# Adding the last two experts' rows in SBUF by one-hot products instead of by scatters to DRAM

## The chip, the cores and the metric

One Trainium2 chip, of which the kernel uses one core. The metric is device time in microseconds (us). Three runs of the kernel before took 2404.68, 2408.65 and 2410.79 us; their median, 2408.65 us, is the time that a change is compared with.

## The reference

Two layers of a diffusion backbone on 512 latent tokens of 1024 channels. The part that matters is the end of the second layer: every token goes to 2 of 8 experts, each expert is a SwiGLU with 3584 hidden units, the results times their gates are added to the stream, and a last norm follows.

```python
top_logit, top_idx = lax.top_k(logits, TOP_K)
gates = jax.nn.softmax(top_logit, axis=-1)
...
hid = jax.nn.silu(xb @ w1[e]) * (xb @ w3[e])
return (hid @ w2[e]) * w[:, None]
...
out = jnp.zeros_like(xt).at[buf_tok].add(y.reshape(P, shp[-1]))
...
x = x + g2 * ffn(h_l)
...
return rmsnorm(x, final_g)
```

All arithmetic is float32. The kernel makes a float32 product of three fast products of the operands' high and low parts.

## The kernel before

The experts are sorted by their number of tokens and have fixed places for 192, 160, 160, 144, 128, 128, 128 and 128 tokens. They are worked on in four pairs: rank 0 with rank 4, 1 with 5, 2 with 6, 3 with 7. In the text the larger expert of a pair is the one of more than 128 tokens, in the last pair 144, and the smaller one has 128.

The weights of an expert stream in blocks of about 1 MB on SP's queue into four buffers `raw`. ScalarE (ACT) rounds each half of a block to its high part `hi`, VectorE (DVE) subtracts to get the low part `lo` (`split`, L165 to L167); each of `hi` and `lo` has five half-block buffers. TensorE (PE) multiplies these. A generator per expert yields after each block, and `weave` takes the generators by turns: first the hidden units (28 blocks for each expert), then the outputs, `outputs` for the smaller expert (14 blocks, called units below, of two 128-row slabs of w2) and `outputs_t` for the larger one (16 steps: four column blocks of 256, each in four steps). The smaller expert comes first in each round, so that the larger one has its last two steps alone.

`outputs` ends with a multiplication by gate and g2 into `yt` (L1339) and a scatter. `outputs_t` ends each column block with a sum of two PSUM halves (`both`, L1287 and L1288), a transposition (`transposed_y`, L1363) and the same multiplication (L1364); after the last column block it issues two scatters, for tokens 0 to 127 and for the 16 that are left. A scatter (L1315) is an indirect DMA of GpSimd (POOL) that adds rows to the stream `xd` in DRAM; the scatters wait for each other.

After the four pairs stands a loop over blocks of tokens beyond the fixed places (L1432), whose count is read from SBUF (L1431). Then `final` (L1452 to L1468) reads the stream back from `xd` in four tiles of 128 tokens, takes squares, root, reciprocal and the product with `final_g`, and writes each tile to the output. A scheduler sets the order of the instructions on each engine, so that the text of the program isn't that order; each engine then works through its own queue in order.

Of the kernel before, what the change touches and what calls it, by code (L numbers as in the profile page):

```python
# [10 lines left out]
F32 = mybir.dt.float32  # L11
# [25 lines left out]
# columns of the constant table  # L37
# [27 lines left out]
# parameters with a value for every channel, as columns of 128 channels  # L65
# [7 lines left out]
def layout(inputs):  # L73
    """The arrays of the launch: the inputs, the parameters as columns, the streams channel-major too, and the constants"""
# [7 lines left out]
    arrays["consts"], arrays["rope"] = const_tables()  # L82
    return arrays


class Net:
# [26 lines left out]
    def slot(self, whole=False):  # L113
        """Buffers (raw, high part, low part) of the next block of the weight stream, by turns; only the raw one if `whole`"""
# [17 lines left out]
    def load(self, src, a, b):  # L132
        """A weight block [128, a, b] (a*b <= 2048): its high and low parts for the fast float32 products."""
# [9 lines left out]
        # in pieces, so that what others wait for can come between  # L143
# [5 lines left out]
    def mm3(self, ps, terms, segs, first=True, last=True):  # L149
        """ps[:, seg] = sum over terms of (wh + wl)^T (xh + xl), without wl^T xl."""  # L150
# [10 lines left out]
    def stream(self, tag, dt, name):  # L161
        """A [128, 8, tokens] tile for the latent tokens and one for the context tokens"""
        return [self.big.tile([P, KT, n], dt, tag=f"{tag}{v}", name=f"{name}{v}") for v, n in enumerate((L, C))]
# [6 lines left out]
    def start(self):  # L170
# [19 lines left out]
        # conditioning vectors: for every k-tile columns (lat, ctx) and zeros, the stationary operand of a quarter of the array  # L190
# [25 lines left out]
    def load_z(self, ss, t):  # L216
        """A tile of x or ctx over its root mean squares, channel-major"""
# [9 lines left out]
    def turn(self, dst, src, t):  # L227
        """A tile of tokens into its place in a channel-major stream"""
# [9 lines left out]
    def first_norm(self, k):  # L238
        """h of layer 0 from the normalised streams, for the channels of k-tile k"""
# [8 lines left out]
    def ada(self, l, t, m=4, before=None, tags=None):  # L248
        """128 m columns of the modulation of layer l from 128 t, in four sums (k-tile modulo 4), in a quarter of the array each"""
# [24 lines left out]
    def columns(self, l, t, m, sums, nv):  # L274
        """Columns t ... of the modulation from their sums and the bias, and the scales times the gains"""
# [40 lines left out]
    def mod(self, l, which):  # L316
        """columns [128, 8, 2] of chunk `which` (sh1, sc1, g1, sh2, sc2, g2) of layer l"""
        return self.acol[l][:, 8 * which:8 * which + 8, :]

    def inv_rms_cols(self, sq, n, d, pool):  # L320
        """1 / sqrt(mean + eps) of the d squares of each of n tokens, whose sums over the partitions of sq [128, n]
        are the squares' sums, as columns of 128 tokens"""
# [9 lines left out]
    def spread(self, r, n, pool):  # L332
        """Columns of 128 tokens as n columns, on every partition"""
# [10 lines left out]
    def norm(self, l, which, seg, pool, out=None, full=None, between=None, tags=None):  # L344
        """The parts of the modulated norm of the stream, for one segment of tokens, into out (or HH, HL)"""
# [27 lines left out]
    def residual(self, k, ps, gate, segs):  # L373
        """x += gate * ps for the channels of k-tile k"""
# [5 lines left out]
    def softplus_cols(self):  # L380
        """n4 = -4 * softplus(-lam), p4 = 4 * softplus(-lam): [128, 16] columns"""
# [10 lines left out]
        V.tensor_tensor(x, x, lam, op=ALU.min)                       # -|lam|  # L392
# [10 lines left out]
        V.tensor_scalar(q, q, 1.0, None, op0=ALU.add)                # exp(f)  # L403
# [914 lines left out]
    def outputs(self, X):  # L1318
# [4 lines left out]
        for u in range(nf // 2):  # L1323
# [10 lines left out]
            if f < nf - 1:  # L1334
                yield
# [203 lines left out]
```

## Time and profile before

| what | value |
|---|---|
| median of three runs | 2408.65 us |
| span of the profiled execution | 2406.2 us |
| PE busy | 2331.3 us, 97% |
| DVE busy | 1733.8 us, 72% |
| ACT busy | 1333.9 us, 55% |
| POOL busy | 43.1 us, 2% |
| HBM read | 477.04 MB |

The profiled execution has no time of its own beside its span; the span, from its first to its last instruction, stands 2.45 us under the median. A matmul counts as busy until its result is written, so that neighbours overlap, and its duration is longer than the distance from one start to the next. "Idle before" is time in which the engine did nothing, and the name behind the arrow is what ended it.

### The profile page before, as it was taken

The numbers are of one execution on the slowest core, as the hardware profiler recorded it, in microseconds if no ns is written. First come the engines' busy times: TensorE is split into PE (matmuls) and PEld (weight loads), VectorE is DVE, ScalarE is ACT, GpSimd is POOL, SyncE is SP. The second block draws the span as 40 slices with busy tenths as digits, with TensorE's granted clock in tenths as the row PEclk, the third lists the DMA queues.
The fourth block names the chain that finished last, engine by engine and source line by source line (L and its number), as shares of the span: only waits on it lengthen the run. The fifth ranks groups of instructions, "written<-read, shape, count | busy, mean of one in ns | idle before, by whom it ended". The sixth has DMA issues, their size and how long they took to land. (4 is left out here: it accounts for less than half of the span.)

```text
span 2406.2 us, 36858 instructions
## 1 busy us (share of the span) xinstructions
PE 2331.3 (97%) x14371; PEld 2058.3 (86%) x14371; DVE 1733.8 (72%) x2620; ACT 1333.9 (55%) x1882; POOL 43.1 (2%) x37
## 2 busy tenths in 40 slices
PE   7999999999999999999799999999999999999995
PEld 5876788888888888898699999999999999999994
DVE  6678786555554456695888877889778887788874
ACT  5687442111212145774566665776667766677763
POOL 0000000000000000000100000000000000100000
PEclk9999999999999999999899999999999999999997
DMA  9255523243332111101788888999899998999995
GB/s 299 84 166 185 166 72 122 84 144 123 123 123 68 39 62 54 36 1 45 260 293 284 297 274 287 316 301 314 287 304 315 304 309 287 310 323 312 306 311 176
DMA packets 349429, 491.10 MB, mean 204 GB/s; under 512 B 8848, under 2 KB 247696, under 8 KB 349248
## 3 DMA queue, kind: packets, MB, share of 16 engines
q1 hardware_dynamic: 346032, 477.50, 59.5%
q0 software_dynamic: 3216, 11.18, 2.0%
q8 instruction: 114, 1.87, 0.3%
q14 instruction: 67, 0.55, 0.1%
HBM read 477.04 MB, written 11.60 MB: 203 GB/s over the span
## 5 line engine op out<-in xcount | busy, mean ns | idle before, releaser
L167 DVE TENSOR_TENSOR lo<-raw,hi 128x1024 fp32r<-128x1024 f32 (+2 forms) x856 | 929.4, 1106 | 252.7 <-ACT hi L166 247.6
L166 ACT ACTIVATE hi<-raw 128x1024 fp32r<-128x1024 f32 (+2 forms) x856 | 803.7, 963 | 482.2 <-PE hb L1282 225.4
L1282 PE MATMUL hb<-XG,hi 128*128 128x320 f32 (+2 forms) x1568 | 428.8, 348 | 0.0
L1280 PE MATMUL hb<-XG,lo 128*128 128x160 f32 (+2 forms) x1792 | 398.6, 242 | 0.0
L1280 PEld LDWEIGHTS hb<-XG,lo 128*128 128x128 f32 x1792 | 332.0, 190 | 4.4
L1282 PEld LDWEIGHTS hb<-XG,hi 128*128 128x128 f32 x1568 | 295.1, 188 | 0.0
L1282 PE MATMUL hb<-HT,hi 128*128 128x320 f32 (+2 forms) x864 | 231.5, 348 | 0.0
L1280 PE MATMUL hb<-HT,lo 128*128 128x160 f32 (+2 forms) x896 | 211.1, 239 | 0.0
L157 PE MATMUL p<-HL,hi 128*128 128x512 f32 (+1 forms) x704 | 192.7, 340 | 0.0
L159 PE MATMUL p<-HH,lo 128*128 128x512 f32 (+1 forms) x704 | 191.0, 338 | 0.0
L155 PE MATMUL p<-HH,hi 128*128 128x512 f32 (+1 forms) x704 | 190.1, 337 | 0.0
L1255 PE MATMUL hb<-hi,XG 128*128 128x512 f32 x448 | 178.0, 397 | 1.8 <-ACT XG L166 1.8
L1256 PE MATMUL hb<-hi,XG 128*128 128x512 f32 x448 | 177.3, 396 | 0.0
L1257 PE MATMUL hb<-lo,XG 128*128 128x512 f32 x448 | 176.9, 395 | 0.0
L1280 PEld LDWEIGHTS hb<-HT,lo 128*128 128x128 f32 x896 | 169.9, 190 | 2.4
L1282 PEld LDWEIGHTS hb<-HT,hi 128*128 128x128 f32 x864 | 162.2, 188 | 1.6
L646 DVE TENSOR_TENSOR sg<-p,sg 128x768 f32<-128x768 f32 (+2 forms) x26 | 21.7, 834 | 153.1 <-PE p L159 153.1
L159 PEld LDWEIGHTS p<-HH,lo 128*128 128x128 f32 x704 | 112.9, 188 | 16.6
L1287 ACT ACTIVATE t<-hb 128x320 f32<-128x320 f32 (+2 forms) x128 | 56.9, 445 | 126.6 <-PE hb L1282 126.6
L155 PEld LDWEIGHTS p<-HH,hi 128*128 128x128 f32 x704 | 112.0, 188 | 15.6
L157 PEld LDWEIGHTS p<-HL,hi 128*128 128x128 f32 x704 | 112.9, 188 | 14.2
L377 DVE SCALAR_TENSOR_TENSOR xT<-py,acol,xT 128x512 f32<-128x512 f32 (+1 forms) x176 | 101.8, 612 | 24.8 <-PE py L159 23.9
(413 smaller groups left out, 4092.9 us busy)
## 6 DMA issues: line engine op xcount, KB each, us to landing
raw<-in_moe_w_dram SPq DMA_DIRECT2D x280, 1024.0 KB, 5.2
raw<-in_moe_w_dram SPq DMA_DIRECT2D x64, 896.0 KB, 5.2
raw<-in_ffn_w_dram SPq DMA_DIRECT2D x33, 1024.0 KB, 5.2
raw<-in_ada_w_dram SPq DMA_DIRECT2D x24, 1024.0 KB, 5.2
araw<-in_ada_w_dram SPq DMA_DIRECT2D x48, 512.0 KB, 3.6
raw<-in_rg_w_in_dram SPq DMA_DIRECT2D x16, 512.0 KB, 6.0
raw<-in_attn_w_qkv_dram SPq DMA_DIRECT2D x6, 1024.0 KB, 5.2
raw<-in_rg_w_out_dram SPq DMA_DIRECT2D x4, 1024.0 KB, 5.4
```

Of the source, the lines that this page charges most:

```text
L155: mm(ps[:, s:e], wh, xh[v][:, s - v * L:e - v * L], start=(first and i == 0), stop=False)
L157: mm(ps[:, s:e], wh, xl[v][:, s - v * L:e - v * L], start=False, stop=False)
L159: mm(ps[:, s:e], wl, xh[v][:, s - v * L:e - v * L], start=False, stop=(last and i == n - 1))
L166: self.nc.scalar.activation(hi, src, AF.Copy)
L167: self.nc.vector.tensor_tensor(lo, src, hi.bitcast(F32), op=ALU.subtract)
L377: self.nc.vector.scalar_tensor_tensor(x, ps[:, s:e], gate[:, k, v:v + 1], x, op0=ALU.mult, op1=ALU.add)
L1255: mm(ps, xh[:, kk], hi[:, k], start=(kk == 0), stop=False)
L1256: mm(ps, xl[:, kk], hi[:, k], start=False, stop=False)
L1257: mm(ps, xh[:, kk], lo[:, k], start=False, stop=(kk == 7))
L1280: mm(ps[:, 0:n], wl, x[:, 0:n], start=False, stop=False)
L1282: mm(ps[:, 0:2 * n], wh, x, start=False, stop=last)
L1287: self.nc.scalar.activation(t, ps[:, :, n:2 * n], AF.Copy)
```

## The change

For the last pair alone (`closing`), the scatters go. When the hidden units of the last pair are done, `held` loads the whole stream from `xd` into four tiles in SBUF (two DMAs of 1 MB on POOL's queue, into the buffers in which the gathered tokens stood) and a table `numbers` of 0 to 511 on every partition (256 KB). `places` compares the table with the token number of each of an expert's rows, which gives a one-hot matrix `S`, `y_parts` splits the rows `yt` into high and low parts, and `combine` multiplies `S` with both parts, for four tiles of 128 tokens, and adds the products to the tiles on DVE. For the larger expert, with rows in two pieces, that is 32 products of 512 columns; for the smaller one 16.

The order of the output products changes in that pair: the larger expert makes four steps first, and then the two go by turns, so that the smaller one has its last two units alone. Its `combine` is marked `last`: after each tile's sum `final` is called for that tile. The loop over further blocks now stands behind that, and `final` reads nothing from DRAM. A root of one number is put behind the larger expert's rows so that ScalarE's table for the root is loaded there. The comments and docstrings are removed too, which changes nothing that is built.

```diff
+    arrays["numbers"] = np.tile(np.arange(L, dtype=np.float32), (P, 1))
...
             V.tensor_tensor(o[:, 1:2], f[:, 0:1], f[:, 2:3], op=ALU.add)
+            V.tensor_tensor(f[:, 7:8], f[:, 0:1], f[:, 2:3], op=ALU.add)
...
+            if self.xs and u == nf // 2 - 2:
+                self.places(X, 0, P)
...
             V.scalar_tensor_tensor(yt[:, ns], ys[:, n], X["idf"][:, 0, 6:7], self.g2b[:, ns], op0=ALU.mult, op1=ALU.mult)
-        self.scatter(X, yt, 0, P)
+            if self.xs:
+                self.y_parts(X, yt, 0, P, ns)
+        if self.xs:
+            self.combine(X, [(0, P)])
+        else:
+            self.scatter(X, yt, 0, P)
...
-            if c == 3:
+            if c == 3 and not self.xs:
                 self.scatter(X, yt[q], q, m)
+            elif c == 3:
+                self.places(X, q, m)
+                self.y_parts(X, yt[q], q, m, slice(0, D))
+                if q:
+
+                    ss = self.mo2.tile([P, 2], F32, tag="ss", name="ss")
+                    self.nc.scalar.activation(ss[:m, 0:1], yt[q][:m, 0:1], AF.Sqrt, bias=self.eps[:m], scale=0.0)
+        if c == 3 and self.xs:
+            self.combine(X, [(0, P), (1, X["n"] - P)])
+
+    def held(self):
+
+        a = self.mo1.tile([P, 2, D], F32, tag="XGa", name="xa")
+        b = self.mo1.tile([P, 2, D], F32, tag="XGb", name="xb")
+        self.xs = [a[:, 0], a[:, 1], b[:, 0], b[:, 1]]
+        for x, j in ((a, 0), (b, 2)):
+            self.nc.gpsimd.dma_start(x, self.xd[j * P:(j + 2) * P, :].rearrange("(j p) d -> p j d", p=P))
+        self.numbers = self.mo2.tile([P, L], F32, tag="sg", name="numbers")
+        self.nc.gpsimd.dma_start(self.numbers, self.I["numbers"])
+
+    def places(self, X, q, m):
+
+        if "S" not in X:
+            X["S"] = self.mo2.tile([P, 2, L], F32R, tag="gx", name="S", bufs=3)
+        self.nc.vector.tensor_scalar(X["S"][:m, q], self.numbers[:m], X["idf"][:m, q, 7:8], None, op0=ALU.is_equal)
+
+    def y_parts(self, X, yt, q, m, ns):
+
+        if q not in X.setdefault("yp", {}):
+            X["yp"][q] = [self.ms.tile([P, D], F32R, tag=t, name="y" + t, bufs=5) for t in ("hi", "lo")]
+        yh, yl = X["yp"][q]
+        self.split(yh[:m, ns], yl[:m, ns], yt[:m, ns])
+
+    def combine(self, X, qs):
+
+        mm = self.nc.tensor.matmul
+        for j in range(4):
+            ps = self.psum()
+            for n in range(2):
+                ts = [(X["S"][:m, q, j * P:(j + 1) * P], y[:m, 512 * n:512 * n + 512]) for q, m in qs for y in X["yp"][q]]
+                for i, (a, b) in enumerate(ts):
+                    mm(ps[:, n], a, b, start=(i == 0), stop=(i == len(ts) - 1))
+            x = self.xs[j]
+            self.nc.vector.tensor_tensor(x, ps.rearrange("p a b -> p (a b)"), x, op=ALU.add)
+            if X.get("last"):
+                self.final(j)
...
         gens = [(self.outputs_t if X["n"] > P else self.outputs)(X) for X in Xs[::-1]]
-        self.weave(gens, 2, turn)
+        if self.closing:
+
+            self.held()
+            for _ in range(4):
+                next(gens[1])
+            self.weave(gens)
+        else:
+            self.weave(gens, 2, turn)
...
-            x = self.ms.tile([P, D], F32, tag="hi", name="x", bufs=5)
-            nc.sync.dma_start(x, self.xd[j * P:(j + 1) * P, :])
...
+        S.activation(o, x, AF.Square, accum_out=ss[:, 0:1])
+        S.activation(ss[:, 1:2], ss[:, 0:1], AF.Sqrt, bias=self.eps, scale=1.0 / D)
+        V.reciprocal(ss[:, 1:2], ss[:, 1:2])
+        V.scalar_tensor_tensor(o, x, ss[:, 1:2], self.fg, op0=ALU.mult, op1=ALU.mult)
+        nc.sync.dma_start(self.out[0, j * P:(j + 1) * P, :], o)
```

On PE, at the end of the program before, the larger expert's products (HT_19834) and their transposition stand last:

```order
L1280 MATMUL hb_22626<-HT_19834,lo_22774 128x144
L1282 MATMUL hb_22626<-HT_19834,hi_22773 128x288
L1363 MATMUL pyt_22808<-ct_75,t0_22805 128x128 x2
L1363 MATMUL pyt_22808<-ct_75,t0_22805 16x128 x2
L1431 TENSOR_LOAD nbi_10257
```

On PE after the change, the one-hot products of the larger expert stand among the last products of the smaller one (HT_19821); hb_22814 and hb_22824 are the sums of the first two token tiles, yhi and ylo the parts of its rows (22800 and 22801 of tokens 0 to 127, 22808 and 22809 of the other 16):

```order
L1333 MATMUL hb_22024<-lo_22785,HT_19821 128x512
L1418 MATMUL hb_22814<-yhi_22800,S_22798 128x512
L1418 MATMUL hb_22824<-yhi_22800,S_22798 128x512
L1418 MATMUL hb_22814<-ylo_22801,S_22798 128x512
L1418 MATMUL hb_22814<-yhi_22808,S_22798 128x512
L1418 MATMUL hb_22824<-ylo_22801,S_22798 128x512
L1418 MATMUL hb_22824<-yhi_22808,S_22798 128x512
L1331 MATMUL hb_22024<-hi_22864,HT_19821 128x512
L1332 MATMUL hb_22024<-hi_22864,HT_19821 128x512
L1418 MATMUL hb_22814<-ylo_22809,S_22798 128x512
```

The smaller expert's last unit (hi_22864) has moved behind the first one-hot products of the larger one, which wait for ACT and DVE to split the rows.

On DVE, at the end of the program before, the larger expert's last sum and the two gate products stand ahead of the loop's count:

```order
L167 TENSOR_TENSOR lo_22770<-raw_22767,hi_22769 128x896
L167 TENSOR_TENSOR lo_22774<-raw_22767,hi_22773 128x896
L1288 TENSOR_TENSOR t0_22805<-hb_22626,t0_22805 128x2x144
L1364 SCALAR_TENSOR_TENSOR yt_21871<-pyt_22808,idf_18114,g2b_10270 128x256
L1364 SCALAR_TENSOR_TENSOR yt_21872<-pyt_22808,idf_18114,g2b_10270 16x256
L1431 TENSOR_LOAD nbi_10257
```

On DVE after the change, four sums into the held tiles xa and xb stand ahead of the smaller expert's rows, and four more behind them, with the last norm (L1527, L1528) at the end:

```order
L1420 TENSOR_TENSOR xb_21861<-hb_22844,xb_21861 128x1024
L1343 SCALAR_TENSOR_TENSOR yt_22884<-hb_22024,idf_18156,g2b_10273 128x512 x2
L168 TENSOR_TENSOR ylo_22887<-yt_22884,yhi_22886 128x512 x2
L1420 TENSOR_TENSOR xa_21860<-hb_22893,xa_21860 128x1024
L1420 TENSOR_TENSOR xa_21860<-hb_22906,xa_21860 128x1024
L1420 TENSOR_TENSOR xb_21861<-hb_22919,xb_21861 128x1024
L1527 RECIPROCAL ss_22899<-ss_22899 128x1
L1420 TENSOR_TENSOR xb_21861<-hb_22932,xb_21861 128x1024
L1528 SCALAR_TENSOR_TENSOR o_22900<-xa_21860,ss_22899,fg_10336 128x1024
L1527 RECIPROCAL ss_22912<-ss_22912 128x1
L1528 SCALAR_TENSOR_TENSOR o_22913<-xa_21860,ss_22912,fg_10336 128x1024
```

The first norm product has moved behind all four of the smaller expert's sums.

## Rows read from the trace of the kernel before

**Rows 1.** Stretch, us, busy of PE, PEld, DVE, ACT, POOL, clock, DMA share, GB/s.

```profile
2340.00:2360.00 20.00, 20.00 (x129) 18.20 (x128) 14.84 (x14) 13.60 (x15) 0.00 (x0) 1.00 0.94 321
...
2390.00:2406.20 16.20, 0.00 (x0) 0.00 (x0) 6.85 (x10) 5.69 (x11) 0.00 (x0) 0.50 0.68 259
```

**Rows 2.** Timeline of the end: start us, us, engine, line, operation, [idle before].

```profile
2355.25 3.45 SPq L1148 DMA_DIRECT2D raw<-in_moe_w_dram  x2
...
2367.10 0.95 ACT L166 ACTIVATE hi<-raw 128x896 fp32r<-128x896 f32 x1 [0.40 <-PE hb L1330]
...
2377.17 0.34 PE L1282 MATMUL hb<-HT,hi 128*128 128x288 f32 x1
...
2377.99 0.46 DVE L1288 TENSOR_TENSOR t<-hb,t 128x288 f32<-128x288 f32 x1 [6.85 <-ACT t L1287]
...
2378.98 0.48 DVE L1364 SCALAR_TENSOR_TENSOR yt<-pyt,idf,g2b 128x256 f32<-128x256 f32 x1 [0.53 <-PE pyt L1363]
...
2379.74 1.55 POOL L1315 DMA_INDIRECT xd<-yt,ids  x1 [8.18 <-DVE yt L1364]
...
2386.82 1.32 POOL L1315 DMA_INDIRECT xd<-yt,ids  x1 [5.53 <-issue]
2390.88 1.78 SPq L1457 DMA_DIRECT2D x<-xd  x4
...
2399.78 1.28 DVE L1467 SCALAR_TENSOR_TENSOR o<-x,ss,fg 128x1024 f32<-128x1024 f32 x1
...
2401.17 1.29 DVE L1467 SCALAR_TENSOR_TENSOR o<-x,ss,fg 128x1024 f32<-128x1024 f32 x1
```

**Rows 3.** Chain of waits at the end: start us, us, what.

```profile
2386.82 3.14 DMA xd<-yt,ids
...
2391.76 6.22 DMA x<-xd
```

**Rows 4.** Timeline of PE in one unit of the smaller expert, its ends.

```profile
2364.39 0.39 PE L1329 MATMUL hb<-hi,HT 128*128 128x512 f32 x1
...
2366.90 0.39 PE L1331 MATMUL hb<-lo,HT 128*128 128x512 f32 x1
```

**Rows 5.** Groups by line and shape, 2280 to 2407 us: count, busy us, mean ns, idle.

```profile
L167 DVE TENSOR_TENSOR lo<-raw,hi 128x1024 fp32r<-128x1024 f32 x26 | 31.2, 1223 | 7.9 <-ACT hi L166 7.9
L166 ACT ACTIVATE hi<-raw 128x1024 fp32r<-128x1024 f32 x26 | 27.2, 1059 | 7.6 <-PE hb L1282 6.8
...
L1339 DVE SCALAR_TENSOR_TENSOR yt<-hb,idf,g2b 128x512 f32<-128x512 f32 x2 | 1.4, 744 | 0.0
...
L167 DVE TENSOR_TENSOR HT<-pht,HT 128x512 fp32r<-128x512 f32 x1 | 0.7, 684 | 0.0
```

**Rows 6.** Groups by line and shape, DVE, the whole span.

```profile
L646 DVE TENSOR_TENSOR sg<-p,sg 128x768 f32<-128x768 f32 x18 | 17.2, 957 | 129.9 <-PE p L159 129.9
...
L301 DVE TENSOR_SCALAR aacc<-araw,cT 128x512 f32<-128x512 f32 x16 | 7.5, 482 | 1.4 <-PE aps L308 1.3
```

**Rows 7.** Waits of ACT, then of SP's queue, 2272 to 2379 us: total, times, longest.

```profile
ACT hi L166 <- PE hb L1282: 24.4, 26, 1.2
...
SPq L1148 <- DVE lo L167: 62.6, 25, 3.9
```

**Rows 8.** DMA issues to landing: 1900 to 1930 us, 1934 to 1950 us; queue q0 there.

```profile
raw<-in_moe_w_dram SPq DMA_DIRECT2D x9, 1024.0 KB, 5.0
...
q0 software_dynamic: 320, 1.11, 23.1%
...
raw<-in_moe_w_dram SPq DMA_DIRECT2D x4, 1024.0 KB, 7.3
```

**Rows 9.** Busy us of each engine in two stretches around that gather.

```profile
1938.00:1945.00 7.00, 7.00 (x52) 6.38 (x52) 6.60 (x19) 4.05 (x6) 2.66 (x3) 1.00 0.80 251
1945.00:1955.00 10.00, 10.00 (x68) 9.37 (x67) 8.88 (x10) 7.25 (x10) 0.00 (x0) 1.00 1.05 367
```

**Rows 10.** Timeline of DVE while a gather is set up.

```profile
1160.75 0.14 DVE L1180 TENSOR_TENSOR idf<-idf 128x1 f32<-128x1 f32 x1
```

More of the change, by code (lines that the diff above doesn't have):

```diff
@@ L1214, in gates, with gathered @@
             V.tensor_tensor(f[:, 6:7], f[:, 3:4], f[:, 5:6], op=ALU.add)
-    def gathered(self, X):
+    def gathered(self, X, tag=None):
         n = X["n"]
-        XG = X["XG"] = self.mo1.tile([P, KT, 2 * n], F32R, tag=f"XG{X['slot']}", name="XG")
+        XG = X["XG"] = self.mo1.tile([P, KT, 2 * n], F32R, tag=tag or f"XG{X['slot']}", name="XG")
         for gx, a, m in X["gxs"]:
@@ L1421, in pair @@
                 return Xs
+            self.xs, self.closing = None, False
             Xs = pair(0, self.rank_gates)
@@ L1428, in moe @@
             for i in range(4):
+                self.closing = i == 3
+                if self.closing:
+                    Xs[1]["last"] = True
                 Xs = self.experts(Xs, (lambda: pair(i + 1)) if i < 3 else None)
+            self.closing = False
             n = nc.values_load(self.nbi[0:1, 0:1], min_val=0, max_val=NX)
@@ L1444, in moe, with final @@
                 X = self.gather("b", pl[:, 0], P)
+                X["last"] = True
                 self.weights(X, e)
                 self.gates(X, pl[:, 1])
-                self.weave([self.gathered(X)])
+                self.weave([self.gathered(X, "HTa")])
                 self.experts([X])
-            self.final()
-    def final(self):
+    def final(self, j):
         nc = self.nc
         V, S = nc.vector, nc.scalar
-        fg = self.fg
-        for j in range(4):
-            x = self.ms.tile([P, D], F32, tag="hi", name="x", bufs=5)
-            nc.sync.dma_start(x, self.xd[j * P:(j + 1) * P, :])
-            ss = self.mo2.tile([P, 2], F32, tag="ss", name="ss")
-            o = self.ms.tile([P, D], F32, tag="lo", name="o", bufs=5)
-            if j == 0:
-                V.scalar_tensor_tensor(o, x, 1.0, x, op0=ALU.mult, op1=ALU.mult, accum_out=ss[:, 0:1])
-            else:
-                S.activation(o, x, AF.Square, accum_out=ss[:, 0:1])
-            S.activation(ss[:, 1:2], ss[:, 0:1], AF.Sqrt, bias=self.eps, scale=1.0 / D)
-            V.reciprocal(ss[:, 1:2], ss[:, 1:2])
-            V.scalar_tensor_tensor(o, x, ss[:, 1:2], fg, op0=ALU.mult, op1=ALU.mult)
-            nc.sync.dma_start(self.out[0, j * P:(j + 1) * P, :], o)
+        x = self.xs[j]
+        ss = self.mo2.tile([P, 2], F32, tag="ss", name="ss")
+        o = self.ms.tile([P, D], F32, tag="lo", name="o", bufs=5)
+        S.activation(o, x, AF.Square, accum_out=ss[:, 0:1])
[3 more added lines that the diff above has]
+        nc.sync.dma_start(self.out[0, j * P:(j + 1) * P, :], o)
     def run(self, upto=9):
```

## The prediction

> **What bounds the kernel now.** I read the busy time by stretch first, since the share over the span hides the end. PE is busy for all 20.00 us of 2340 to 2360 us and for none of 2390 to 2406.2 us [rows 1]. So there are two parts with different limits: a stream of products bound by PE, and a tail without products.
>
> In the stream I looked at who waits. ACT waits for PE to free a high-part buffer, never for a weight, and SP's queue spends 62.6 us in 25 waits for DVE to free a raw buffer [rows 7]. Weights are there early; what PE is given to do decides.
>
> For the tail I read the timeline and the chain of waits. The last product starts at 2377.17 and ends at 2377.51. Then come sum, transposition and gate product, the first scatter at 2379.74, the second at 2386.82 [rows 2], which lands 3.14 us later at 2389.96; SP's reads of the stream start at 2390.88, and the wait for them takes 6.22 us from 2391.76 [rows 3]. The last norm product ends at 2401.17 + 1.29 = 2402.46, the span at 2406.2. From the last product to the end: 28.7 us, of which two scatters and the reading back, from 2379.74 to 2397.98, are 18.2 us. That is all that the change can remove.
>
> **What the change removes.** These 18.2 us. Below I count what takes their place, from one moment: the end of the larger expert's last product, called E. The stream's weight products are the same in number. Their order puts the smaller expert's last two units behind E. A unit has 12 products; the first and last of them start 2.51 us apart [rows 4], so 0.228 us each. 24 of them are 5.47 us, and with an equal stream E is at 2377.51 - 5.47 = 2372.04.
>
> **What it adds, along DVE after E.** In this tail DVE is the engine with most to do.
>
> 1. Until the larger expert's rows stand. ACT's copy and the sum end 0.94 after E, as before (2377.51 to 2378.45). The transposition is put behind six of the smaller expert's products, until about E + 1.2; transposition 0.4, gate product 0.48 [rows 2]: E + 2.1.
> 2. Split and table. ACT rounds 1024 columns in 1.06 [rows 5], until E + 3.2, then the 16 further rows; DVE subtracts twice. One takes 1.22 [rows 5]; I use 1.2 for each such pass that follows another, since neighbours overlap a little: E + 5.6. The smaller expert's one-hot matrix costs 0.48 by the comparable one-operand row [rows 6]; its last unit's two splits 2.4: E + 8.4.
> 3. The larger expert's four sums. Such a sum, 1024 columns with one operand in PSUM, isn't in the trace. The nearest is 957 ns for 768 columns [rows 6], and 0.46 us for 288 [rows 2]; the slope gives 1.22, the split of 1024 gives 1.2. I take 1.2; the ends are 0.96 (as if 1024 cost no more than 768) and 1.37 (two of the 684 ns halves [rows 5]). Two sums: E + 10.8. The third and fourth wait for PE: with three buffers in PSUM, of which the smaller expert holds one, the third group of eight products starts only when the first sum has been read, at E + 9.7, takes 8 x 0.228 + 0.16 until its result stands, and its sum ends at E + 12.9. The fourth group ends at E + 13.5, its sum at E + 14.7.
> 4. The smaller expert's last three products come behind those groups in PE's queue and end at E + 14.2, under that sum. Its rows: two gate products, 1.4 [rows 5], and two half subtractions of 0.68, 1.4: E + 17.5.
> 5. Its one-hot products: most are done while DVE works; the last adds 0.4. Three sums, reciprocal, fourth sum: 4 x 1.2 + 0.1: E + 22.8. ACT's square of the first tile (1.06 by ACT's pass over 1024 columns [rows 5]) and its root hide under the second and third sum.
> 6. Four norm products, each with a reciprocal: 1.39 from start to start [rows 2]: E + 28.4.
> 7. The end. Before, 3.74 us lie between the last norm product and the span's end. The loop's barrier, formerly ahead of the reads (2389.96 to 2390.88: 0.92 us [rows 2, 3]), now comes behind the output's landing: 4.66 together. E + 33.0.
>
> 2372.04 + 33.0 = 2405.1. The tail that I remove and the tail that I add are alike, because DVE's eight sums, four row splits and the norm follow each other where before a DMA was waited for. Added early: one more 128x1 instruction per gathered group, 12 in all at 0.14 us or less [rows 10]. Of those only the first three delay anything (the first weights wait for that DVE chain): 0.2 us. The others lie where PE is busy anyway. Loading the table of the root moves into the stream, where ACT is busy 13.60 of 20 us [rows 1]: nothing, and without that cover 1.3 us. Span: 2405.3 against 2406.2, **0.9 us less**. On the median of the runs, 2408.65, this gives 2407.8.
>
> **What the held loads cost.** They are 2.36 MB more on POOL's queue, issued when the larger expert has its four steps in a row, just after the hidden units. Such a step takes 3.42 us (three of them lie between the last product of a unit at 2366.90 [rows 4] and that of the stream at 2377.17, 10.27 us), four 13.7 us, and they need 3.67 MB (four blocks of 896 KB): 267 GB/s. The stretch 1945 to 1955 shows 367 GB/s with PE never idle [rows 9]. So 13.7 us carry 5.0 of the 6.0 MB wanted; 1.0 MB is late, 2.7 us. Raw blocks land some 4 us before their first use: the last of before is issued at the end of a pair that takes 3.45 us from 2355.25, so at about 2358.3, lands 5.0 us later [rows 8], and ACT reads it from 2367.10 on [rows 2]. Behind it stand five split halves. I take no stall. Ends: none, and 2.36 MB at the 321 GB/s of the stream [rows 1], 7.4 us. An earlier episode bears on it: a gather of 1.11 MB on that queue made weight blocks land in 7.3 instead of 5.0 us [rows 8], and PE was busy throughout [rows 9].
>
> The Trainium skill, "DMA: Bandwidth & Descriptors", section "Queues, rings and completion order", speaks against the change here: each DMA engine takes turns between the queues that have work, a packet at a time. By it the held loads would have half of the engines until they are done, about 2 x 2.36 MB / 367 GB/s = 12.9 us, and the weights 184 GB/s in place of 267: 1.1 MB or 2.9 us late, an estimate from that page and the row above it. The sum would still hold, since 2.9 is under 4.
>
> **Rivals.**
> - *Held loads starve PE* (slower). Mechanism and place: the weight stream falls behind at 2285 to 2300 us and PE waits; it decides once blocks are over 4 us late and the split halves are used up. Price up to 7.4 us; with the forecast 2415.2. For it: a DMA share of 0.94 in the stream [rows 1], so there is little to catch up with. Against it: rows 7 to 9. Slower by more than 0.3% only if all of it shows together with longer waits of PE for the splits at E + 3 to 10. Chance 0.10.
> - *DVE never waits* (faster). Without the waits in steps 1 to 3 and with the barrier under the landing, 3.6 + 0.9 us go: 2403.3, which is still within 0.3%. To be over that, the larger expert's sums would also have to vanish under the last two units (4.8 us more: 2398.5). The order speaks against it, as these sums stand after the last split. Chance of over 0.3%: 0.06.
> - *The clock falls*. In the tail before PE has 0.50, the 1.2 GHz level [rows 1], after no products. If it fell in the gap of some 2 us before the smaller expert's one-hot products, or in the waits before, at most the last 8 + 3 + 16 products would take twice 0.228: 6 us, of which most lies under DVE's sums; about 2 us, 2409.8. Within the forecast's class.
> - *The change does not do what it says*: if the loop ran, the scatter would be left out of it too, but the trace shows no products after 2379.9 us, so it runs zero times, and it adds only its barrier.
>
> **How the numbers follow.** 0.3% of 2408.65 is 7.2 us, about what a measurement can tell from no change (the three runs spread over 6.1 us). No measurable change: 0.84, for the forecast and the small versions of the rivals; faster 0.06; slower 0.10. The range: below, DVE without waits and barrier (4.5 us) and sums at 0.96 (8 x 0.24 = 1.9 us) would give 2401.4 if both held; above, 7.4 us of starvation would give 2415.2. Taking off the unlikely ends and adding the spread of the runs, 2402.5 to 2413.5.
>
> **What would show it right or wrong.** Right: no POOL scatter in the last pair; PE's last product some 18 us after E and some 10 us from the norm's end; DVE busy almost throughout from E + 3 on; the chain of waits ending in L1528, L1420 and one output DMA instead of `xd`. Step 3 is wrong if the third and fourth sum don't wait for PE; step 7, if the span ends less than 4 us after the last L1528. The forecast is wrong if PE has gaps between 2283 and E, or if E isn't near 2372.

## The result and the profile after

The changed kernel takes 2421.13 us (median of four runs, 2417.06 to 2426.99) against 2408.61 us for the kernel before in the same session. The ratio is 1.0056, 95% interval 1.0043 to 1.0069: it is slower by half a per cent, where the forecast was 2407.8 us and no measurable change.

The profiled execution is the longest of the four, 2426.99 us with a span of 2425.0. It is compared with the kernel before from E on, the end of the larger expert's last product, as in the prediction. E is at 2376.91, 4.87 us behind the forecast 2372.04. Of these, 4.67 us are already there when the first expert's weights are multiplied (near 1204 us): 2.7 us by 370 us, where nothing was changed, and most of the rest around 1160 to 1190 us, where the clock was at 0.5 for 30.7 us in this execution and for 23.9 us in that of the kernel before. This early shift differs from execution to execution (-1.5 to +5.4 us over the profiles below, against the profile of the kernel before, whatever the edit), so tails are compared from E.

The kernel before ends 28.69 us after its last product; with the two units that now stand behind E (5.47 us) that is **E + 34.2**. The changed kernel ends at **E + 48.1**. The 13.9 us between the two are what has to be explained; the forecast was E + 33.0.

Busy time by stretch in the changed kernel, columns as in [rows 1]: the stretch of the held loads, the stream, the way from E to the smaller expert's last product (24.24 us), and that way cut where the clock changes.

```profile
2290.00:2300.00 10.00, 10.00 (x83) 10.00 (x83) 7.03 (x8) 5.70 (x7) 0.00 (x0) 1.00 1.04 390
2340.00:2360.00 20.00, 20.00 (x130) 18.15 (x129) 15.30 (x16) 13.16 (x15) 0.00 (x0) 1.00 0.91 315
2376.91:2401.15 24.24, 23.65 (x60) 12.15 (x59) 11.33 (x12) 4.31 (x5) 0.00 (x0) 0.71 0.00 1
2376.91:2383.57 6.66, 6.07 (x24) 3.43 (x23) 4.76 (x7) 4.31 (x5) 0.00 (x0) 1.00 0.00 0
2383.57:2393.81 10.24, 10.24 (x21) 5.42 (x19) 4.12 (x4) 0.00 (x0) 0.00 (x0) 0.50 0.01 2
```

The first two rows answer to [rows 1, 9]: the held loads raise the traffic to 390 GB/s and PE has no gap. The rows after E show the loss: PE is the busy engine (23.65 of 24.24 us), not DVE, and the clock falls to 1.2 GHz 6.66 us after E, with PE at work for 6.07 of these. In the 10.24 us that follow PE gets through 21 products.

PE and its weight loads (PEld) in the timeline of the changed kernel, in the first one-hot products, still at 2.4 GHz:

```profile
2381.50 0.19 PEld L1418 LDWEIGHTS hb<-ylo,S 128*128 128x128 f32 x1 [0.96 <-DVE ylo L168]
2381.51 0.49 PE L1418 MATMUL hb<-ylo,S 128*128 128x512 f32 x1 [0.53 <-DVE ylo L168]
2381.93 0.18 PEld L1418 LDWEIGHTS hb<-yhi,S 16*128 16x128 f32 x1 [0.24 <-issue]
2381.93 0.49 PE L1418 MATMUL hb<-yhi,S 16*128 16x512 f32 x1
2382.35 0.19 PEld L1418 LDWEIGHTS hb<-ylo,S 128*128 128x128 f32 x1 [0.24 <-issue]
2382.35 0.49 PE L1418 MATMUL hb<-ylo,S 128*128 128x512 f32 x1
```

Products of 128 and of 16 stationary rows alternate here, and each starts 0.42 us after the one before; in [rows 4] it was 0.228. The weight load of each starts together with its product, not beside the one before.

DVE at the end of the changed kernel, timeline: the larger expert's third and fourth sum, then the smaller expert's sums and norm.

```profile
2395.98 1.23 DVE L1420 TENSOR_TENSOR xb<-hb,xb 128x1024 f32<-128x1024 f32 x1 [4.86 <-PE hb L1418]
2399.61 1.23 DVE L1420 TENSOR_TENSOR xb<-hb,xb 128x1024 f32<-128x1024 f32 x1 [2.40 <-PE hb L1418]
2401.19 1.41 DVE L1343 SCALAR_TENSOR_TENSOR yt<-hb,idf,g2b 128x512 f32<-128x512 f32 x2 [0.35 <-PE hb L1333]
...
2406.53 2.36 DVE L1420 TENSOR_TENSOR xa<-hb,xa 128x1024 f32<-128x1024 f32 x2 [2.55 <-PE hb L1418]
...
2414.20 1.28 DVE L1528 SCALAR_TENSOR_TENSOR o<-xb,ss,fg 128x1024 f32<-128x1024 f32 x1
...
2415.60 1.28 DVE L1528 SCALAR_TENSOR_TENSOR o<-xb,ss,fg 128x1024 f32<-128x1024 f32 x1
```

DVE waits for PE before these sums, 4.86 and 2.40 us before the third and fourth, and 2.55 us before the smaller expert's first. From the end of the last norm product, 2416.88, to the span's end, 2425.0, are 8.1 us, against 3.74 in [rows 2]. The instruction records show what lies there: the engines meet at the loop's exit until 2420.9, POOL's drain lasts from 2421.01 to 2423.45, SP passes the exit until 2424.02, and the closing exchange follows. Before, the same 2.44 us drain lay at 2391.15, beside SP's reading of the stream. In the instruction records of the loop's line, the drains of POOL's queue (count, shortest, median and longest in ns, first and last start), in the kernel before and in the changed one:

```profile
L1535 POOLq DRAIN  x3: 46/109/2437, 2391.1 to 2405.9; - x3
```

```profile
L1596 POOLq DRAIN  x3: 46/109/2437, 2421.0 to 2424.8; - x3
```

### The profile page after: what moved, and what is told of

The parts are those of the page before. It is cut to its first block, busy times and chain, and to the rows that moved or that the text cites. A ratio compares the mean times of both kernels' runs of the same rounds, so it can differ in the third digit from the quotient of the medians.

```text
span 2425.0 us, 36982 instructions
## 1 busy us (share of the span) xinstructions
PE 2356.8 (97%) x14419; PEld 2072.9 (85%) x14419; DVE 1747.5 (72%) x2645; ACT 1338.9 (55%) x1889; POOL 41.8 (2%) x37
## 4 chain that ended last, share of the span: by engine, by line
PE 93%; ACT 3%; DVE 2%; DMA 1%; issue 0%; SPq 0%; ACTq 0%; DVEq 0%
PE hb L1284 19%; PE hb L1282 9%; PE p L158 5%; PE p L160 5%; PE p L156 5%; PE hb L1258 4%; PE hb L1259 4%; PE hb L1257 4%; PE py L156 3%; PE py L158 3%; PE py L160 3%; PE hb L1331 2%; PE hb L1333 2%; PE hb L1332 2%; PE hb L1281 2%; PE po L160 1%
## 5 line engine op out<-in xcount | busy, mean ns | idle before, releaser
L156 PEld LDWEIGHTS p<-HH,hi 128*128 128x128 f32 x704 | 112.0, 188 | 15.6
L158 PEld LDWEIGHTS p<-HL,hi 128*128 128x128 f32 x704 | 112.9, 188 | 14.2
L378 DVE SCALAR_TENSOR_TENSOR xT<-py,acol,xT 128x512 f32<-128x512 f32 (+1 forms) x176 | 102.0, 613 | 24.7 <-PE py L160 23.9
```

The costliest lines, as they stand in the source:

```text
L156: mm(ps[:, s:e], wh, xh[v][:, s - v * L:e - v * L], start=(first and i == 0), stop=False)
L158: mm(ps[:, s:e], wh, xl[v][:, s - v * L:e - v * L], start=False, stop=False)
L378: self.nc.vector.scalar_tensor_tensor(x, ps[:, s:e], gate[:, k, v:v + 1], x, op0=ALU.mult, op1=ALU.add)
```

## The experiments

There are four theories of where the time went. **A**: one-hot products cost more than 0.228 us because of the 16-row piece, directly and by the clock. **B**: PE's waits behind E bring the clock down, whatever the products are. **C**: the loop's exit, now behind the output, takes longer. **D**: the new order costs it.

The numbers of the runs on these theories are in one table. E is as above, S the end of the smaller expert's last product, all in us, of one profiled execution each; "clock" is the granted clock from E to S. Medians, and ratios to the kernel before with intervals, are of all executions (4 to 12 each).

| kernel | S - E | clock | last norm product - S | end - that | end - E | median | ratio |
|---|---|---|---|---|---|---|---|
| before (with two units added) | | | | | 34.2 | 2408.4 to 2410.1 | |
| changed | 24.2 | 0.71 | 15.7 | 8.1 | 48.1 | 2421.13 | 1.0056 [1.0043, 1.0069] |
| e1 order only | 6.0 | 1.00 | 26.6 | 3.7 | 36.3 | 2410.23 | 1.0006 [0.9997, 1.0015] |
| e2 no 16-row products | 14.6 | 1.00 | 14.1 | 7.9 | 36.6 | 2412.80 | 1.0012 [1.0003, 1.0021] |
| e3 waits filled | 26.7 | 0.68 | 13.9 | 8.2 | 48.8 | 2423.22 | 1.0052 [1.0038, 1.0066] |
| e4 no loop | 24.8 | 0.69 | 15.6 | 3.7 | 44.1 | 2418.62 | 1.0038 [1.0024, 1.0051] |
| e6 grouped | 15.8 | 1.00 | 14.1 | 7.8 | 37.7 | 2417.24 | 1.0036 [1.0022, 1.0049] |
| e14 the same again | 21.1 | 0.71 | 15.6 | 8.0 | 44.8 | 2415.80 | 1.0022 [1.0009, 1.0034] |
| e8 padded to 128 rows | 14.6 | 1.00 | 16.0 | 7.7 | 38.3 | 2414.25 | 1.0022 [1.0013, 1.0031] |
| e11 grouped, no loop | 17.3 | 0.90 | 14.1 | 3.7 | 35.2 | 2412.62 | 1.0012 [1.0002, 1.0022] |
| e13 padded, no loop | 14.6 | 1.00 | 14.5 | 3.7 | 32.9 | 2406.68 | 0.9992 [0.9983, 1.0001] |

**e1, the order alone.**

```diff
+AHEAD = 4
...
+        if self.closing:
+            for _ in range(AHEAD):
+                next(gens[1])
+            self.weave(gens)
```

> The kernel before with one edit: in the last pair the larger expert's output steps run four ahead, so the smaller expert's products end last; scatters, reading back and norm are as in the kernel before. E is the end of the larger expert's last product. If the lost time lies in the one-hot products, the order alone costs little: POOL's scatters in the kernel before start 7.1 us apart, so the three start at about E+2.4, E+9.5 and E+16.6, against E+14.8 for the last one before, and the time is 2408.6 + 1.8 = about 2410 us (2406 to 2412). If the order is what costs (two units of the smaller expert back to back, waits for weights), about 2419 to 2421 us.

Measured: 2410.23 us, ratio 1.0006, no difference that can be told; the tail is 2.1 us longer than that of the kernel before. D falls as the cause of the 13.9 us. POOL and the reading in that run's timeline:

```profile
2375.54 1.55 POOL L1316 DMA_INDIRECT xd<-yt,ids  x1 [268.73 <-DVE yt L1365]
2382.33 1.32 POOL L1316 DMA_INDIRECT xd<-yt,ids  x1 [5.24 <-DMA xd<-yt,ids]
2387.19 1.56 POOL L1316 DMA_INDIRECT xd<-yt,ids  x1 [3.54 <-issue]
...
2394.26 1.77 SPq L1466 DMA_DIRECT2D x<-xd  x4
```

A scatter of 128 rows holds up the next step for 6.8 and 7.1 us, the one of 16 rows for 4.9. I had taken 7.1 for each.

**e2, without the 16-row products.**

```diff
-            self.combine(X, [(0, P), (1, X["n"] - P)])
+            self.combine(X, [(0, P)])
```

> The changed kernel without the one-hot products of the larger expert's last 16 rows: those 16 rows are not added to the stream; all else stays, so 16 of the 32 products of the first combination go and no row count alternates. Theory A (the alternation of pieces of 128 and 16 rows makes each product 0.33 to 0.57 us): the remaining 16 take 0.23 us at 2.4 GHz, the smaller expert's last product ends at E+11 instead of E+24.2 and the time is about 2408 to 2410 us. Theory B (the short waits after E bring the granted clock to 0.5, whatever the rows): the clock still falls near E+7, the 16 remaining products and what follows take 0.43 us each, the last product ends near E+18 and the time is about 2414 to 2416 us. Rival C (the end behind the output alone): 2420 us.

**e3, the waits filled.**

```diff
+        if not getattr(self, "after_pairs", False):
+            pf = self.tr.tile([P, 512], F32, tag="tr", name="pfill")
+            for i in range(18):
+                mm(pf[:, 0:256], X["HT"][:, i, 0:P], X["HT"][:, i, 0:256], start=True, stop=True)
         for j in range(4):
```

> The changed kernel with 18 more products of 256 columns into a spare PSUM tile that nobody reads, ahead of each of the two combinations, so that TensorE works through the waits for the split rows (about 2 us each time). Theory B (the waits bring the clock down): the granted clock stays at 1.00 until the smaller expert's last product, the one-hot products take 0.33 to 0.42 us instead of 0.57 and the last product ends near E+17 to E+19; the time is about 2413 to 2415 us. Theory A (the clock falls because of what the one-hot products themselves are): the clock falls as before, and the time is 2421 to 2424 us.

Measured: 2412.80 and 2423.22 us. These two belong together. Busy time of e2 from E to S:

```profile
2375.14:2389.76 14.62, 11.03 (x44) 6.97 (x43) 11.07 (x12) 4.32 (x5) 0.00 (x0) 1.00 0.01 2
```

Busy time of e3 from E to the fall of its clock, and from E to S:

```profile
2372.55:2399.25 26.70, 26.70 (x81) 15.82 (x80) 11.32 (x12) 4.32 (x5) 0.00 (x0) 0.68 0.00 1
2372.55:2381.36 8.81, 8.81 (x44) 5.82 (x43) 5.53 (x8) 4.32 (x5) 0.00 (x0) 1.00 0.01 2
```

e2 leaves PE idle for 3.6 of 14.6 us and keeps 2.4 GHz to S; e3 never lets it idle and falls to 1.2 GHz at E + 8.8. So the clock fell without a wait and held through one of 2.85 us: B is out as the account of this fall, as far as one profiled execution of each can show it. e2's S is 3.6 us later than expected, since PE waits 2.85 us for the last unit's split on DVE, which stands behind the larger expert's sums.

**e4, without the loop.**

```diff
-            n = nc.values_load(self.nbi[0:1, 0:1], min_val=0, max_val=NX)
-            with tc.For_i(0, n, 1) as it:
...
-                self.experts([X])
```

> The changed kernel without the loop over further blocks of tokens, which runs no turn for these inputs. Theory C (the loop's exit and POOL's 2.4 us drain, which lay beside the reading back in the kernel before, now stand behind the last output): the span ends about 3.5 us earlier, about 2417.5 us. Theories A and B alone: the loop costs nothing at the end and the time stays at 2420 to 2422 us.

Measured: 2418.62 us, 2.5 less than the changed kernel across sessions, and the two ratios' intervals overlap; but in the trace it is 3.7 us from the last norm product to the end instead of 8.1. C holds for 4.4 us in the traces. The last norm product and the last output in that run's timeline (span 2416.9):

```profile
2411.86 1.28 DVE L1508 SCALAR_TENSOR_TENSOR o<-xb,ss,fg 128x1024 f32<-128x1024 f32 x1
2413.17 0.33 SPq L1509 DMA_DIRECT2D out_dram<-o  x1
```

**e6 and e14, grouped by piece; e8, padded.** What about the 16-row products is it: the change of row count, or the rows? e6 and e14 are one kernel.

```diff
-        for j in range(4):
-            ps = self.psum()
-            for n in range(2):
-                ts = [(X["S"][:m, q, j * P:(j + 1) * P], y[:m, 512 * n:512 * n + 512]) for q, m in qs for y in X["yp"][q]]
...
+        for j0 in (0, 2):
+            pss = [self.psum() for _ in range(2)]
+            for i, (q, m) in enumerate(qs):
+                for j in range(2):
+                    for n in range(2):
```

> The changed kernel with the same one-hot products in another order: for two groups of 128 tokens together first the eight products of the 128-row piece, then the eight of the 16-row piece, so that the row count changes 3 times in the first combination instead of 15. E is the end of the larger expert's last product. If the change of row count is what costs (weights not loaded ahead), the 128-row products take 0.23 us, the clock stays at 1.00 as it did without the 16-row products, and the smaller expert's last product ends at E+18 to E+19: about 2414 us. If the 16-row products themselves bring the granted clock down, whatever their order, the clock falls again some 5 us into them and the last product ends near E+22 to E+24: 2419 to 2421 us.

> The grouped kernel profiled a second time. If the grouping holds the granted clock at 1.00 in every execution, its tail is E+37.7 again and the rest of its time is a late E. If the clock falls in some executions, this one may show a stretch at 0.5 between E+7 and E+23 and a tail of E+39 to E+43.

```diff
+        V.memset(idf[:, 1, 7:8], -1.0)
...
+        if self.closing:
+            self.nc.gpsimd.memset(yt[1], 0.0)
...
-            self.combine(X, [(0, P), (1, X["n"] - P)])
+            self.combine(X, [(0, P), (1, P)])
```

> The changed kernel with the larger expert's 16-row piece filled up with zero rows to 128: as many one-hot products (32), all of 128 rows. If it is the row count that slows them and brings the clock down, every product takes 0.23 us, the clock stays at 1.00, the smaller expert's last product ends at E+14.6 + 16 x 0.23 = E+18.3 and the span at E+40.3, that is 6 us above the kernel before (E+34.2 on the same scale): about 2415.5 us. If the number of products with little else to do is what brings the clock down, it falls as in the changed kernel: 2420 us or more.

Measured: 2417.24 and 2415.80 us grouped, 2414.25 padded. S is at E + 14.6 in e8, 3.7 us sooner than expected: the 16 added products lie where PE waited in e2, and PE is busy for 14.03 of the 14.63 us. PE and PEld in e8 at the same products as shown above for the changed kernel:

```profile
2378.90 0.19 PEld L1421 LDWEIGHTS hb<-yhi,S 128*128 128x128 f32 x1
2379.13 0.39 PE L1421 MATMUL hb<-yhi,S 128*128 128x512 f32 x1
2379.14 0.19 PEld L1421 LDWEIGHTS hb<-ylo,S 128*128 128x128 f32 x1
2379.37 0.39 PE L1421 MATMUL hb<-ylo,S 128*128 128x512 f32 x1
```

With one row count each weight load starts beside the product before, and products start every 0.23 us. PE in e6, where the piece changes once and then 16-row products follow each other:

```profile
2383.49 0.40 PE L1419 MATMUL hb<-ylo,S 128*128 128x512 f32 x1
2383.82 0.18 PEld L1419 LDWEIGHTS hb<-yhi,S 16*128 16x128 f32 x1 [0.36 <-ACT hi L167]
2383.82 0.49 PE L1419 MATMUL hb<-yhi,S 16*128 16x512 f32 x1
2384.15 0.39 PE L1419 MATMUL hb<-ylo,S 16*128 16x512 f32 x1
2384.39 0.39 PE L1419 MATMUL hb<-yhi,S 16*128 16x512 f32 x1
```

The distance from start to start is 0.33 us on either side of the change and 0.24 between 16-row products after that: here it is the change of row count that is dear, not the few rows. Between E and S the changed kernel has 18 such changes and the grouped one 6. At full clock the 6 cost e6 1.2 us against e8, 0.2 each; by that the 18 are some 3.5 us (an estimate) of the 9.6 us by which the changed kernel's S is later than e8's, and some 6 us are left for the clock. The Trainium skill, "TensorE: Matmul & The Clock Gate", section "Architectural detail: the array is 16× 32×32, not 1× 128×128", says that PE's queue can pull weight loads ahead of products in flight. The traces agree while the row count stays (the load 0.23 us ahead of its product in e8) and show a case where it did not happen: at a change of the row count the load starts together with its product.

The clock is another matter. The two profiles of the grouped kernel, busy time from E to S, e6 first and then e14:

```profile
2377.62:2393.42 15.80, 15.21 (x61) 9.77 (x59) 11.14 (x12) 4.32 (x5) 0.00 (x0) 1.00 0.01 2
```

```profile
2374.88:2395.99 21.11, 20.52 (x61) 12.89 (x59) 11.23 (x12) 4.32 (x5) 0.00 (x0) 0.71 0.01 1
```

The same instructions: in one execution at 2.4 GHz throughout, in the other at 1.2 GHz from E + 9.05 on. So the fall alone is worth 7.1 us (end at E + 44.8 against 37.7). With 16-row products it isn't certain but likely: before S it came in five of the six profiles that have them (changed, e3, e4, e11, e14; not e6), and in none of the three with only 128-row products (e2, e8, e13). But 16-row products aren't needed for a fall. In e8, after S, PE waited 1.99 us for the smaller expert's rows, and soon after the clock was at 0.5 for 3.4 us:

```profile
2391.10:2394.50 3.40, 3.40 (x9) 2.64 (x9) 1.07 (x3) 0.27 (x1) 0.00 (x0) 0.50 0.00 0
```

That cost some 1.4 us, by the way from S to the last norm product (16.0 against 14.5 in e13, which has the same wait and no fall).

**e13 and e11, both away.** Padded as in e8, or grouped as in e6, and without the loop as in e4 (the diffs above together).

> The changed kernel with the 16-row piece filled up with zero rows to 128 and without the loop over further blocks, which runs no turn for these inputs: both suspects away, the rest as changed. If the row count (with the clock) and the loop's exit are all of the loss, the span ends at E+38.3-4.4 = E+33.9 us, E the end of the larger expert's last product, against E+34.2 in the kernel before: about 2409 us, no difference that can be told. If a third cost is hidden, it shows here: 2412 us or more.

> The changed kernel with the one-hot products grouped by piece and without the loop over further blocks, which runs no turn for these inputs. By the traces the two should bring the end to E+33.3, E the end of the larger expert's last product (E+37.7 with the grouping, less 4.4 for the loop), 0.9 us under the kernel before: about 2408 to 2409 us, with the granted clock at 1.00 until the last product. The grouped run's executions were 4.5 us longer than its trace's tail explains: if the grouping holds the clock only in some executions, or something else of the change costs, this run is at 2412 to 2413 us.

Measured: 2406.68 us padded, 0.9992 [0.9983, 1.0001], no difference that can be told. The span ends at E + 32.9, 15.2 us sooner than in the changed kernel: 9.6 of them before S, 1.2 from S to the norm, 4.4 behind the norm. A and C together account for all of the loss. e8 and e13 differ by the loop alone, and their ratios' intervals lie apart, so that C shows in the times too, though not its size. Grouped: 2412.62 us (2405.42 to 2416.51), with the clock at 0.5 for 3.4 us in the profile. Part of that spread may be what the clock does from one execution to the next, as in e6 and e14, and part the early shift; only one execution was profiled, so this isn't shown.

**e5, e9, e10, e12: towards a faster version.** The scatters of the larger expert can lie beside products if it runs further ahead. (e7, an earlier form of e9, left out eight of the larger expert's sixteen output steps; its 2374.97 us say nothing.)

e5 is e1 with eight steps instead of four, and the transposition's block and tile are fixed when it is queued:

```diff
+AHEAD = 8
...
-                    self.pending.append(lambda: self.transposed_y(X, c, t, yt))
+                    self.pending.append(lambda c=c, t=t: self.transposed_y(X, c, t, yt))
```

> The kernel before with one edit: in the last pair the larger expert's output steps run eight ahead instead of in turn, so that six units of the smaller expert follow its last product and both its scatters (7.1 us apart) land beside them; one scatter of the smaller expert is left behind the last product, and nothing is summed in SBUF. S is the end of the last product. In the kernel before the second scatter started 9.3 us behind it and the span ended 19.4 us after that; now the scatter can start at S+1.8 and the span ends at S+21.2 instead of S+28.7: about 2402 us (2401 to 2404). If six units of the smaller expert back to back (1 MB in 2.7 us, 383 GB/s) wait for weights, S is later by up to 4 us: 2406. If the order itself cost as much as it saves: 2409.

e9 loads the stream when the larger expert has ended and its scatters are issued. Its root for ScalarE's table, which stood behind the larger expert's rows, now reads `fg`:

```diff
+        ss = self.mo2.tile([P, 2], F32, tag="ss", name="ss")
+        self.nc.scalar.activation(ss[:, 0:1], self.fg[:, 0:1], AF.Sqrt, bias=self.eps, scale=0.0)
...
+            for _ in range(8):
+                next(gens[1])
+            while next(gens[1], self) is not self:
+                next(gens[0])
+            next(gens[0])
             self.held()
-            for _ in range(4):
-                next(gens[1])
-            self.weave(gens)
+            self.weave(gens[:1])
```

> The larger expert eight steps ahead in the last pair, its rows scattered to DRAM as in the kernel before; then the stream is loaded into SBUF and only the smaller expert's 128 rows are added by one-hot products. S is the end of the smaller expert's last product. With the clock at 1.00 until the last one-hot product the way from S to the span's end is that of the run without the 16-row products, 22.0 us, against 28.7 in the kernel before: about 2402.5 us (2401 to 2405). The second scatter should land near S-3.4 and the stream by S+3.6, just before the first sum wants it at S+3.8; each us that it comes later is on the path. Rival: one-hot products of any kind bring the clock down, then 2405 to 2406 us.

e10 moves the norm:

```diff
-                if self.closing:
-                    Xs[1]["last"] = True
...
                 self.experts([X])
+            for j in range(4):
+                self.final(j)
```

> The run with the larger expert eight ahead and one expert combined, with the final norm moved behind the loop over further blocks, so that the loop's exit comes after the sums and not after the outputs are on their way. If the 4.4 us by which the run without the loop was shorter are the loop's exit waiting for the outputs and POOL's drain behind it, they go; against that the four norms no longer start beside the sums, about 2.5 us. Sum: 2 us faster than the run with the norm ahead of the loop, about 2400.5 us. If the loop costs as much wherever it stands, it is 2 to 4 us slower than that run, about 2405 us.

In e9 that root ran at 1182 us, long before the end, and the table was loaded again at 2383.9, behind the norm's first square. e12 loads it behind the larger expert's scatters:

```diff
                 self.scatter(X, yt[q], q, m)
+                if self.closing and q:
+                    ss = self.mo2.tile([P, 2], F32, tag="ss", name="ss")
+                    self.nc.scalar.activation(ss[:m, 0:1], yt[q][:m, D - 1:D], AF.Sqrt, bias=self.eps[:m], scale=0.0)
```

> The run with the larger expert eight ahead and one expert combined, with the table for the square root loaded on ACT beside the last units instead of after the first square, where it took 1.28 us of the chain (ACT_TABLE_LOAD 1.28 at the end of that run's trace). S, the end of the smaller expert's last product, to the span's end: 22.0 - 1.3 = 20.7 us; 2403.8 - 1.3 = about 2402.5 us, 0.25 per cent under the kernel before. If the end is held by something that does not wait for the norms (the loop's exit by itself), it stays at 22.0 us and 2403.8.

| kernel | S to end, us | median, us | ratio to before |
|---|---|---|---|
| before (S: its last product) | 28.7 | 2408.4 to 2409.3 | |
| e5 eight ahead, all by scatters | 24.1 | 2404.46 | 0.9980 [0.9970, 0.9989] |
| e9 eight ahead, smaller one in SBUF | 22.0 | 2403.83 | 0.9983 [0.9973, 0.9992] |
| e10 as e9, norm behind the loop | 22.3 | 2404.22 | 0.9979 [0.9970, 0.9987] |
| e12 as e9, table early | 22.4 | 2404.17 | 0.9979 [0.9971, 0.9988] |

All four beat the kernel before by some 0.2%, and the changed kernel by more, and can't be told from each other. e5 does it by the order alone. POOL and SP in e5:

```profile
2375.39 2.07 POOL L1316 DMA_INDIRECT xd<-yt,ids  x1 [5.75 <-DVE lo L168]
...
2382.66 1.56 POOL L1316 DMA_INDIRECT xd<-yt,ids  x1 [5.20 <-DVEq L1441]
...
2389.74 1.78 SPq L1466 DMA_DIRECT2D x<-xd  x4
```

The last scatter starts 1.7 us after S as expected, but the reading starts 7.1 us later, not 4.1: behind the kernel before's last scatter, of 16 rows, it was 4.06 (2386.82 to 2390.88 in [rows 2]), and this one has 128. So e5 misses its forecast by 2.5 us (2404.46 against 2402; the tail by 2.9). e9's tail is the expected 22.0. In both, S lies about 1 us later than the last product of the kernel before when the early shift is taken off; why, I didn't separate. e10 misses: the first square and the first reciprocal in its timeline:

```profile
2389.37 1.06 ACT L1529 ACTIVATE o<-xa 128x1024 f32<-128x1024 f32 x1 [6.65 <-DVEq L1502]
...
2393.20 0.16 DVE L1531 RECIPROCAL ss<-ss 128x1 f32<-128x1 f32 x1 [4.21 <-ACT ss L1530]
```

Against e9 the way behind the last norm product is 4.0 us shorter, but that from S to it is 4.3 us longer, since the norm waits for the loop's exit. e12 misses too, DVE in its timeline:

```profile
2386.20 0.15 DVE L1533 RECIPROCAL ss<-ss 128x1 f32<-128x1 f32 x1
2386.27 1.21 DVE L1423 TENSOR_TENSOR xb<-hb,xb 128x1024 f32<-128x1024 f32 x1
2387.39 1.28 DVE L1534 SCALAR_TENSOR_TENSOR o<-xa,ss,fg 128x1024 f32<-128x1024 f32 x1
```

The first norm product waits for the sums on DVE, not for the root: the table's 1.28 us had cover.

## Why the prediction was wrong

- **The stream, E, the held loads**: right, but for the early shift of E. No gap of PE between 2283 us and E, 390 GB/s where the loads run; the two loads of the stream land 9.3 and 9.0 us after their issue, beside weights. The table `numbers`, which the sum put among them, was loaded 23 us earlier. The rule of the Trainium skill, "DMA: Bandwidth & Descriptors", section "Queues, rings and completion order", by which weights might come 2.9 us late, was of no consequence, as the sum had it. The trace agrees with it in kind: weight blocks of 1 MB that land beside the held loads take 7.6 us, against 5.0 in [rows 8].
- **Steps 1 and 2**: right to 0.1 us. The 128 rows stand at E + 2.1; the row splits end at E + 5.7 (5.6), the last unit's splits at E + 8.3 (8.4); the one-hot table takes 0.47.
- **Step 3, the step that failed**: the term 8 x 0.228 for a group of one-hot products. The 0.228 comes from products that all have 128 stationary rows [rows 4]; half of the larger expert's one-hot products have 16, and I didn't ask what a change of row count costs, nor what the clock does there. They started every 0.42 us at 2.4 GHz, later every 0.57 us on the mean at 1.2 GHz. The sums are sized right (1.22 us each, forecast 1.2), but DVE waits for PE, 10.7 us in all in four waits ahead of the larger expert's sums, where the sum had PE waiting for DVE in the third and fourth group. My sign for step 3 asked only whether the third and fourth sum wait for PE; they did, for another reason.
- **Step 4**: the last products at E + 24.2 instead of E + 14.2. With 128-row products only, e8 and e13 put them at E + 14.6, so that the structure of the sum stands and the price of the products, with the clock that goes with it, was off.
- **The rival "the clock falls"** came true, with a wrong place and price. I tied it to the wait ahead of the smaller expert's products and let DVE's sums hide most of it: 2 us. It fell already at E + 6.7, in the larger expert's products, where e2, e3 and e8 tie it to the 16-row products and not to waits, and it is worth 7.1 us in the grouped kernel. What I did name, a fall at the gap before the smaller expert's products, is what e8 shows, for 1.4 us.
- **Steps 5 and 6**: sizes right. The four norm products take 5.7 us from the last sum on, forecast 5.6. The smaller expert's first sum starts 5.3 us after its gate product's start instead of 3.2, while its one-hot products ran at 1.2 GHz.
- **Step 7**: 8.1 instead of 4.66. I moved the loop's exit behind the output with the 0.92 us that it shows in [rows 2, 3]. There it had been under a DMA's landing: POOL's drain of 2.44 us and SP's pass through the exit were hidden and not in that number.
- **The rest of the forecast**: with the two costs away e13 ends at E + 32.9, where the forecast was E + 33.0. That it fits to 0.1 us is luck: e13 has no loop, so that its end is 0.9 us shorter than step 7, and S and the way from S to the norm are 0.4 and 0.3 us longer than in the sum. The gain of 0.9 us isn't shown, since e13's time can't be told from that of the kernel before.
- **Range and chances**: the slower side had 0.10, for starving loads alone. A new kind of product on the bounding engine had no bound above 0.228 us at full clock, though no row that I read showed one of 16 rows. The trace of before has eight, short transpositions of 16 columns at 2018.3 us; they give no price for the change, since the 0.34 us from the first to the second product behind them are nearly the 0.31 us behind 128-row transpositions at 2025.8.

## What to carry to other kernels

Price a new matmul by its stationary rows and by its neighbours, not by the columns alone; where short pieces would alternate with full ones, filling them up with zeros (e8) was cheaper here than grouping them (e6, e14). Work that leaves a DMA's shadow uncovers what else lay in that shadow, here a loop's exit, so look at every instruction between the old place and the end. If a slow step can be started earlier under the stream, the order alone (e5) may give as much as replacing it.

## What the hardware showed that was not expected

- A product whose stationary operand has another row count than the one before started 0.42 us after it at 2.4 GHz where every product changes, and at a single change the distances on both sides of it were 0.31 to 0.34 us (e6); in a run of 512-column products of one row count they were 0.23 to 0.24, for 16 rows as for 128. Each change adds some 0.2 us (e6 against e8).
- The granted clock fell to 0.5 with PE without idle time (e3: 8.81 of 8.81 us busy) when 16-row products were among its work, and held at 1.00 with PE idle for a quarter of the time (e2: 11.03 of 14.62 us) when they were not. Two executions of one kernel differ in it (e6, e14), and e8 had a stretch at 0.5 without any such product, behind a wait of 1.99 us that left e13 at 1.00. What exactly brings it down stays open.
- An indirect scatter holds the next step on the stream for about 7 us with 128 rows and 4 to 5 us with 16.
- The exit of a loop that runs no turn costs 4.4 us when it stands behind the last output (e4, e13).
